# Opening projections accumulated block by block as the conditioning arrives, in a two-layer hybrid backbone

## The chip, the cores and the metric

The kernel runs on one core of a Trainium2 chip. The metric is the device time of one execution in microseconds, as a median over runs; a profiled execution is shown beside it.

## The reference

Two layers over 512 latent tokens and 256 context tokens (768 together), width 1024, in fp32. Each layer has two sub-layers, and each reads a normalised input that is modulated by vectors computed from the conditioning:

```python
mod = jax.nn.silu(c) @ w_ada[layer] + b_ada[layer]            # 1024 -> 6144, and the same for c_ctx
sh1, sc1, gt1, sh2, sc2, gt2 = jnp.split(mod[:, None, :], 6, axis=-1)
h = rmsnorm(x, g_norm1[layer]) * (1 + sc1) + sh1              # the same for the context, with its own mod
p = jnp.split(h @ w_in[layer], SPLIT_POINTS, axis=-1)         # one combined input projection
ya = window_attention(...)    # A: banded attention with rotary
yb = dense_attention(...)     # B: dense attention, normalised q and k, rotary
ym = mlstm_mixer(...)         # C
yd = mamba_mixer(...)         # D
x = x + gt1 * (concat(ya, yb, ym, yd) @ w_out[layer])
h2 = rmsnorm(x, g_norm2[layer]) * (1 + sc2) + sh2
x = x + gt2 * (square(relu(h2 @ w_ff1[layer])) @ w_ff2[layer])
```

So nothing of the input projection can start before the shift and scale (`sh1`, `sc1`) are there. They are the first 2048 columns of `mod`, and the weights for them are 8 MB.

## The kernel before

Activations lie feature-major: `x` is eight chunks of 128 features by 768 tokens (`CTX` the first 256, `LAT` the other 512), held in four double chunks `xr[q]`. Every fp32 operand of a projection is split into a rounded part and a rest (`h`/`hl` for activations, `wh`/`wl` for weights), and a product is three matmuls: high by high, high by low, low by high. `feat` gives a feature-major result of 128 outputs, `tok_group` a token-major one of 128 tokens; each runs over all eight chunks of the contraction and holds one PSUM tile `bulk` (two buffers). `granule(g)` loads 256 output columns of `w_in` through `wload`: DMA into `wraw` (four buffers), ScalarE rounds into `wh`, VectorE subtracts into `wl` (six buffers each). PSUM has besides `bulk` the tags `mx` (two buffers of one bank) and `s2` (two buffers of two banks). Most large tiles share twelve SBUF slots by role (`k6`).

The opening of layer 0. SP issues small constants, then the four loads of `x` (`start_x`), then the conditioning weights. `rms_row` squares on ScalarE, adds on VectorE, sums over partitions by matmuls with ones, and `x` is scaled in place by the row. Then for q = 0 to 3 two sums (`ada_first`) give shift and scale of two chunks. A sum takes 256 columns of `mod` over eight chunks: eight matmuls of 256 columns, each in one of four groups of 32 array columns (`ada_rows`); a ScalarE copy; two transposes, a reduction and the bias (`ada_cols`). Chunks 2q and 2q+1 are then modulated and split into `hs`. After all four rounds the projections run, each over the whole contraction: values for A and B (`G_ABV`, six token groups), keys of A (`G_ABK`), queries of A (`G_AQ`, two halves), each evacuated as it ends (`rotate` applies the rotary by four ScalarE copies of 32 partitions, POOL and VectorE; `put_k` and `put_q` split).

The remaining projections are cut into a stream of small matmul groups (`Stream`, `fill`) that is fed into the attention and scan code by credits. The sixteen other sums of layer 0 (`ada0_step`, columns of `gt1`, `sh2`, `sc2`, `gt2`) are steps in that order: two before and one after the queries of A, six in the stream beside attention A (credit 2.0 each), three and three in the streams beside D and C, one at the end. Each issues its own four loads into `ada` (three buffers), at a priority that lets SP take them as gaps come.

The sums for layer 1 (`ada_step`) run in layer 0's feed-forward on ScalarE and POOL: four loads, ScalarE multiplies by the conditioning, POOL adds (line 292, 294), and at the next step (`ada_finish`) TensorE sums over partitions (line 95, `bulk<-ones,acc`). Of the feed-forward loops `ffn1(b)` calls a step with its second weight block, for b under 2 with its first as well; `ffn2(b)` calls two. All 24 are done before the last pass.

A tile framework orders each engine's instructions by program order and readiness; queues are in order.

Of the kernel before, what the change touches and what calls it, by code (L numbers as in the profile page):

```python
# [43 lines left out]
def tile_hybrid_backbone(ctx, tc, xin, cin, wada, win0, win, wout, wf1, wf2, pcol, prow, cst, rope, out):  # L44
# [77 lines left out]
    SY.dma_start(cc, cin)  # L122
    SY.dma_start(cs, cst)
# [11 lines left out]
    pcs, prs, mods = [], [], []  # L135
    for l in range(DEPTH):
        pcs.append(T((P, NPC), name="pcol"))
        prs.append(T((P, NPR), name="prow"))
        mods.append(T((P, 2, 48), name="mod"))
        SY.dma_start(pcs[l], pcol[l])  # L140
        SY.dma_start(prs[l], prow[l:l + 1, :].to_broadcast([P, NPR]))
# [5 lines left out]
    sth = sm((P, 8, 2), "sth")  # L147
# [28 lines left out]
    def rsq(out_, src, scale, eps):  # L176
        n = src.shape[1]
        v = sm((P, 24), "rv", bufs=2)[:, 0:n]
        y = sm((P, 24), "ry", bufs=2)[:, 0:n]
        w = sm((P, 24), "rw", bufs=2)[:, 0:n]  # L180
# [10 lines left out]
    XIN_ROLES, XOUT_ROLES = (3, 9, 10, 11), (3, 4, 0, 11)  # L191
# [3 lines left out]
    xr = [k6(r, (P, 2, NT), name="x") for r in XIN_ROLES]  # L195
# [4 lines left out]
    def ada_rows(o, kr):  # L200
        for k, w in kr:
            g = slice(32 * (k % 4), 32 * (k % 4) + 32)
            mm(o[g, :], silw[:, 2 * k:2 * k + 32], w, k < 4, k >= 4)

    def ada_cols(l, cb, row, oc):
        for m in range(2):
            TE.transpose(oc[:, m * P:(m + 1) * P], row[:, m * P:(m + 1) * P], ident)
        r = sm((P, 2, 2), "adr", bufs=2)
        V.tensor_reduce(r, oc.rearrange("p (m g i v) -> p v m g i", m=2, g=4, v=2)[:, :, :, :, 0], AX.X, ALU.add)
        tt(mods[l][:, :, 2 * cb:2 * cb + 2], r,  # L210
           pcs[l][:, C_BADA + 2 * cb:C_BADA + 2 * cb + 2].unsqueeze(1).to_broadcast([P, 2, 2]), ALU.add)

    def ada_first(i, cb):
        pt_ = s2()
        o, oc = pt_[:, 0, 0:256], pt_[:, 1, 0:256]
        for kh in range(2):
            if i == 7:
                raws = [T((P, 2, 256), F32, "wraw", 4) for _ in range(2)]
                for q in range(2):
                    SY.dma_start(raws[q], wada[0, cb, kh][:, 2 * q:2 * q + 2, :])  # L220
                ada_rows(o, [(4 * kh + k, raws[k // 2][:, k % 2, :]) for k in range(4)])
            else:
                raw = k6(raw_roles[(2 * i + kh) % 8], (P, 4, 256), name="adaw")
                SY.dma_start(raw, wada[0, cb, kh])
                ada_rows(o, [(4 * kh + k, raw[:, k, :]) for k in range(4)])
        row = tf((P, 256), name="adarow")
# [4 lines left out]
    ada0 = {"i": 8, "pend": None}  # L231

    def ada0_finish():
        if ada0["pend"] is not None:
            cb, row = ada0["pend"]
            ada_cols(0, cb, row, bulk((P, 256)))
            ada0["pend"] = None

    def ada0_step(gate=None):
# [4 lines left out]
        with ExitStack() as st:  # L244
            st.enter_context(tc.high_priority(offset=-1000000))
            if gate is not None:
                st.enter_context(tc.issue_after(gate))
# [3 lines left out]
        o = bulk((P, 256))  # L251
        ada_rows(o, [(k, raws[k // 2][:, k % 2, :]) for k in range(8)])
        row = T((P, 256), F32, "adrow", 2)
        act(row, o, AF.Copy)
        ada0["pend"] = (cb, row)
        ada0["i"] = cb + 1
# [48 lines left out]

    def feat(W, m, acts, sl):
        o = bulk((P, sl.stop - sl.start))
# [177 lines left out]
    for l in range(DEPTH):  # L485
# [11 lines left out]
        if l == 0:  # L497
            hs = new_h()
            def start_x():
                for q in range(4):  # L500
                    SY.dma_start(xr[q], xin[:, 2 * q:2 * q + 2, :])
                for sl in (LAT, CTX):
                    row = rms_row(lambda c: xr[c // 2][:, c % 2, sl], sl.stop - sl.start)
                    for c in range(8):
                        xv = xr[c // 2][:, c % 2, sl]
                        tt(xv, xv, row, ALU.mult)

            start_x()
            for q in range(4):
                for i in range(2):  # L510
                    ada_first(2 * q + i, (4 + q, q)[i])
                for sl, v in ((LAT, 0), (CTX, 1)):
                    s = norm_scale(l, v, C_G1, 8, slice(2 * q, 2 * q + 2))
                    for c in (2 * q, 2 * q + 1):
                        xv, hv = xr[c // 2][:, c % 2, sl], hs[c][0][:, sl]
                        sc, sh = s[:, c:c + 1], md[:, v, c:c + 1]
                        act(hv, xv, AF.Identity, bias=sh, scale=sc)
                        ts(xv, xv, sc, sh, ALU.mult, ALU.add)
                        (G if (c + v) % 2 == 0 else V).tensor_tensor(hs[c][1][:, sl], xv, hv.bitcast(F32), ALU.subtract)
# [180 lines left out]
        W = granule(G_ABV)  # L700
        VS = {a: k6(r, (P, 2, NJ, P), F32R, name="VS") for a, r in (("A", 4), ("B", 5))}
        for j in first_tok:
            o = tok_group(W, j, hs, 256)
            ov = o.rearrange("p (a b v) -> p a b v", a=2, b=2)
            for ai, a in enumerate("AB"):
                act(VS[a][:, :, j, 0:64], ov[:, ai], AF.Copy)
                tt(VS[a][:, :, j, 64:128], ov[:, ai], VS[a][:, :, j, 0:64].bitcast(F32), ALU.subtract)
        W = granule(G_ABK, 0)
        khl["A"] = [k6(r, (P, 2, NT), F32R, name="KHL") for r in (6, 7)]
        pl = feat(W, 0, hs, LAT)  # L710
        put_k(rotate(pl, None, tf((P, NL), name="ra"), rp), khl["A"], LAT)
        put_k(feat(W, 0, hs, CTX), khl["A"], CTX)
        W = granule(G_AQ)
        if l == 0:
            ada0_step(gate=last_dma[0])
            ada0_step()
        for m in range(2):
            eos["A", m] = k6((8, 0)[m], (P, 2, NT), F32R, name="EO")
        for m, sl in snake(segs_out):
            pp = feat(W, m, hs, sl)  # L720
# [16 lines left out]
        def gates():  # L737
            X = sm((P, NJ, 16), "X")
# [92 lines left out]
        astep = [g_do(ada0_step, 2.0)] if l == 0 else []  # L831
        t_ada = 2.0 * len(astep)
# [20 lines left out]
        def ev_conv(i, m, sl):  # L853
            def run(pp):
# [13 lines left out]
                [g_tok(j, hs, 280, ev_z(j)) for j in first_tok] + [gstep] + astep)]  # L868
        for i, g in enumerate((G_DX, G_DB, G_DC)):
# [3 lines left out]
            gs = gs[:len(od) // 2] + [gstep] + (astep if i < 2 else []) + gs[len(od) // 2:] + [gstep]  # L873
            grs.append((lambda g=g: granule(g), gs + astep))
        stream.start(grs, 6 * 2.8 + 4 * (t_lat + t_ctx) + 2 * (t_lat + (t_ctx if need else 0)) + 6 * t_ada)
# [644 lines left out]
```

## Time and profile before

| | |
|---|---|
| median of three runs | 1907.8 us (1907.74 to 1911.45) |
| profiled execution | 1914.86 us, span 1913.1 us |
| TensorE busy | 1796.9 us, 94% of the span |
| VectorE, ScalarE, POOL busy | 1229.7, 869.0, 335.3 us |
| granted TensorE clock, mean | 0.97 |
| DMA | 178.83 MB, mean 93 GB/s |

TensorE's busy time counts pipelined matmuls, so what it stands still is read from waits and from the granted clock by stretches, not from the share. A row of the timeline gives start, length, engine, line, operation and tiles, and in brackets the idle time before it with what ended it. Line 95 is the matmul helper, 103 the activation helper, 106, 110, 111 and 114 VectorE helpers.

### The profile page before, as it was taken

What the parts mean: (1) busy time and instruction counts of PE and PEld (TensorE: products, weight loads), DVE (VectorE), ACT (ScalarE), POOL (GpSimd) and SP (SyncE); (2) the same over time, 40 slices, a digit from 0 to 9 for tenths busy, and PEclk for the clock granted to TensorE, in tenths of its full rate; (3) what the DMA queues carried; (4) which work ended last, traced back from release to release, by engine and by line L of the source; (5) the groups of instructions that cost most, each with busy time, mean ns of one, the idle gap of its engine ahead of it and who ended that gap; (6) DMA issues with size and microseconds to landing.
All of it is one profiled execution on the core that took longest, in us unless ns stands there. A gap on an engine that the chain in (4) does not pass through costs nothing.

```text
span 1913.1 us, 30450 instructions
## 1 busy us (share of the span) xinstructions
PE 1796.9 (94%) x11370; PEld 1552.7 (81%) x11370; DVE 1229.7 (64%) x2811; ACT 869.0 (45%) x1822; POOL 335.3 (18%) x321
## 2 busy tenths in 40 slices
PE   5899999998999899999999999998998899999997
PEld 2687888777878788888888877988877699999997
DVE  6547768478874456645655657787578765555556
ACT  3445532355655555433543436553355543333333
POOL 1210013031004454412412402013120100000000
PEclk9899999999999899999999999999989999999999
DMA  7413243332013234323423321122222022322322
GB/s 265 128 63 111 68 133 108 102 96 99 28 34 119 80 119 129 113 86 116 130 86 104 116 89 58 35 90 67 78 77 67 28 83 92 98 98 89 97 91 67
DMA packets 98100, 178.83 MB, mean 93 GB/s; under 512 B 10784, under 2 KB 19360, under 8 KB 97952
## 3 DMA queue, kind: packets, MB, share of 16 engines
q1 hardware_dynamic: 97952, 176.88, 28.7%
q8 instruction: 90, 1.47, 0.3%
q14 instruction: 58, 0.48, 0.1%
HBM read 172.51 MB, written 4.33 MB: 92 GB/s over the span
## 4 chain that ended last, share of the span: by engine, by line
PE 77%; DVE 8%; ACT 5%; DMA 4%; issue 3%; POOL 2%; SPq 0%; DVEq 0%; ACTq 0%; POOLq 0%
PE bulk L95 40%; PE s L95 26%; PE mx L95 8%; PE mx L658 2%; DMA CB<-drows 1%; DMA ada<-in_wada_dram 1%; DMA adar<-in_wada_dram 1%; POOL acc L292 1%; ACT wh L103 1%; DVE wl L106 1%; ACT qs L103 1%; DMA adaw<-in_wada_dram 1%; DMA wraw<-in_wout_dram 1%; ACT adap L103 1%; DVE x L114 0%
## 5 line engine op out<-in xcount | busy, mean ns | idle before, releaser
L103 ACT ACTIVATE wh<-wraw 128x512 fp32r<-128x512 f32 (+2 forms) x400 | 241.2, 612 | 306.4 <-PE bulk L95 152.4
L106 DVE TENSOR_TENSOR wl<-wraw,wh 128x512 fp32r<-128x512 f32 (+2 forms) x400 | 282.5, 712 | 114.0 <-ACT wh L103 105.1
L95 PE MATMUL s<-h,wh 128*128 128x258 f32 (+2 forms) x1024 | 311.6, 314 | 0.0
L95 PE MATMUL s<-hl,wh 128*128 128x258 f32 (+2 forms) x1024 | 301.1, 312 | 0.0
L95 PE MATMUL s<-h,wl 128*128 128x258 f32 (+2 forms) x1024 | 247.4, 313 | 0.0
L95 PE MATMUL bulk<-ah,wh 128*128 128x512 f32 (+1 forms) x576 | 218.7, 380 | 1.1 <-DVE x L114 0.6
L114 DVE SCALAR_TENSOR_TENSOR x<-bulk,mod,x 128x512 f32<-128x512 f32 (+1 forms) x224 | 149.6, 672 | 107.0 <-PE bulk L95 106.4
L95 PE MATMUL bulk<-al,wh 128*128 128x512 f32 (+1 forms) x576 | 217.2, 377 | 0.0
L95 PE MATMUL bulk<-ah,wl 128*128 128x512 f32 (+1 forms) x576 | 216.9, 376 | 0.0
L292 POOL TENSOR_TENSOR acc<-acc,adap 128x512 f32<-128x512 f32 x96 | 141.3, 1479 | 413.3 <-ACT acc L103 220.7
L95 PEld LDWEIGHTS s<-h,wh 128*128 128x128 f32 x1024 | 195.5, 191 | 20.7
L95 PEld LDWEIGHTS s<-hl,wh 128*128 128x128 f32 x1024 | 195.7, 191 | 11.4
L95 PE MATMUL bulk<-h,wh 128*128 128x512 f32 (+1 forms) x448 | 166.3, 371 | 2.1 <-DVE fD L114 0.7
L95 PEld LDWEIGHTS s<-h,wl 128*128 128x128 f32 x1024 | 164.2, 191 | 1.3
L95 PE MATMUL bulk<-hl,wh 128*128 128x512 f32 (+1 forms) x448 | 156.9, 350 | 0.0
L95 PE MATMUL bulk<-h,wl 128*128 128x512 f32 (+1 forms) x448 | 156.8, 350 | 0.0
L95 PEld LDWEIGHTS bulk<-ah,wh 128*128 128x128 f32 x576 | 109.1, 189 | 21.8 <-DVE mod L106 1.3
L95 PEld LDWEIGHTS bulk<-ah,wl 128*128 128x128 f32 x576 | 108.9, 189 | 21.2
L95 PEld LDWEIGHTS bulk<-al,wh 128*128 128x128 f32 x576 | 108.8, 189 | 19.5
L95 PE MATMUL bulk<-wh,h 128*128 128x256 f32 (+1 forms) x368 | 115.3, 315 | 6.3 <-DVE fD L114 3.2
L103 ACT ACTIVATE relu<-relu,bs 128x512 f32<-128x512 f32 x96 | 59.0, 647 | 117.3 <-DVE relu L106 117.1
L95 PE MATMUL bulk<-wl,h 128*128 128x256 f32 (+1 forms) x368 | 110.0, 300 | 2.0 <-DVE wl L106 1.9
(329 smaller groups left out, 3786.5 us busy)
## 6 DMA issues: line engine op xcount, KB each, us to landing
wraw<-in_wf_dram SPq DMA_DIRECT2D x256, 256.0 KB, 2.8
adar<-in_wada_dram SPq DMA_DIRECT2D x96, 256.0 KB, 3.1
wraw<-in_win_dram SPq DMA_DIRECT2D x80, 256.0 KB, 2.9
ada<-in_wada_dram SPq DMA_DIRECT2D x64, 256.0 KB, 3.4
wraw<-in_wout_dram SPq DMA_DIRECT2D x32, 256.0 KB, 2.9
adaw<-in_wada_dram SPq DMA_DIRECT2D x14, 512.0 KB, 10.5
x<-in_xin_dram SPq DMA_DIRECT2D x8, 768.0 KB, 6.0
CB<-drows SPq DMA_DIRECT2D x10, 512.0 KB, 6.1
```

Source lines behind the costliest of these rows:

```text
L95: return TE.matmul(o, lhsT=l, rhs=r, start=start, stop=stop)
L103: return S.activation(o, i, f, scale=scale, **kw)
L106: return V.tensor_tensor(o, a, b, op)
L114: return V.scalar_tensor_tensor(o, a, s, b, op0, op1)
L292: G.tensor_tensor(acc[:, v], acc[:, v], dst, ALU.add)
L658: TE.transpose(tp[:, i, e, :], Ps[e][:, (i0 + i) * P:(i0 + i + 1) * P], ident)
```

## The change

1. `x` is loaded first; the constants are issued between its parts, layer 1's columns after the first round.
2. The root mean square: ScalarE squares, TensorE sums directly with ones in four groups of 32 columns over all chunks, two ScalarE copies, four transposes, one reduction and `rsq` for both token kinds, six matmuls that spread the row, two ScalarE copies into `rowx`. `x` is no longer scaled in place; `norm_chunk` multiplies by scale and row, adds the shift and splits; odd chunks on POOL.
3. A conditioning sum takes sixteen matmuls of 128 columns in four groups instead of eight of 256; its result is 128 by 128, with one transpose.
4. The first projections run per block q of the contraction: two chunks' worth of values for A and B, keys of A and the first half of the queries of A, into `pav` and `pf`, which hold both `s2` and both `bulk` buffers. Their weights come in a new array `wopen`, one load pair per block. In program order the conditioning of round q+1 stands ahead of block q's matmuls. The second half of the queries follows in `mx`, after the evacuations are issued.
5. The later sums of layer 0: `ada0_load` issues the four loads (four buffers) ahead of `ada0_step`; `spread` places loads and steps evenly in the streams (eight beside A, three, three), credit 1.2 each; one step stands before attention A.
6. The sums of layer 1: a step per `ffn1(b)` for every b, two per `ffn2(b)`, so the last two fall into the last `ffn2`.
7. Small tiles: one buffer instead of two in `rsq`, `bs` two instead of four, `X` and `sth` in shared tags.

```diff
+    for q in range(4):
+        SY.dma_start(xr[q], xin[:, 2 * q:2 * q + 2, :])
+        if q == 0:
+            SY.dma_start(cc, cin)
+        if q == 1:
+            SY.dma_start(cs, cst)
+        if q == 2:
+            load_cols(0)
...
-    def ada_rows(o, kr):
-        for k, w in kr:
-            g = slice(32 * (k % 4), 32 * (k % 4) + 32)
-            mm(o[g, :], silw[:, 2 * k:2 * k + 32], w, k < 4, k >= 4)
+    def ada_rows(o, k, w):
+        for g in range(4):
+            i, m = g % 2, g // 2
+            mm(o[32 * g:32 * g + 32, :], silw[:, 2 * (k + i):2 * (k + i) + 32], w[:, i, m * P:(m + 1) * P], k == 0, k == 6)
...
+    def ada0_load():
+        cb = ada0["i"]
+        if cb < 24 and ada0["raws"] is None:
+            ada0["raws"] = [T((P, 2, 256), F32, "ada", 4) for _ in range(4)]
+            for q in range(4):
+                SY.dma_start(ada0["raws"][q], wada[0, cb, q // 2][:, 2 * (q % 2):2 * (q % 2) + 2, :])
...
-            raws = [T((P, 2, 256), F32, "ada", 3) for _ in range(4)]
-            for q in range(4):
-                SY.dma_start(raws[q], wada[0, cb, q // 2][:, 2 * (q % 2):2 * (q % 2) + 2, :])
...
+            ssq = mx()
...
+            for q in range(4):
+                sq = [k3((P, NT), F32, name="sq") for _ in range(2)]
+                for i in range(2):
+                    act(sq[i], xr[q][:, i, :], AF.Square)
+                for i in range(2):
+                    for g, sl in ((i, LAT), (2 + i, CTX)):
+                        mm(ssq[32 * g:32 * g + 32, 0:sl.stop - sl.start], ones.to_broadcast([P, 32]), sq[i][:, sl], q == 0, q == 3)
...
+            pav, pf = [s2(), bulk()], [s2(), bulk()]
+
+            def cond(q):
                 for i in range(2):
                     ada_first(2 * q + i, (4 + q, q)[i])
-                for sl, v in ((LAT, 0), (CTX, 1)):
+
+            cond(0)
+            load_cols(1)
+            for q in range(4):
+                for i, (sl, v) in enumerate(((LAT, 0), (CTX, 1))):
                     s = norm_scale(l, v, C_G1, 8, slice(2 * q, 2 * q + 2))
                     for c in (2 * q, 2 * q + 1):
...
+                        norm_chunk(xr[c // 2][:, c % 2, sl], sl, s[:, c:c + 1], md[:, v, c:c + 1], rows[i], *hs[c], pool=c % 2 == 1)
+                W = wload([wopen[i, q] for i in range(2)])
+                WT, WF = W[:2], W[2:]
+                if q < 3:
+                    cond(q + 1)
+                else:
+                    ada0_load()
+                for k in (2 * q, 2 * q + 1):
+                    ah, al = hs[k]
+                    h, lo = WT[k % 2]
+                    for j in first_tok:
...
+                        mm(o, ah[:, js], h, k == 0 and j % 2 == 0, False)
+                        mm(o, ah[:, js], lo, False, False)
+                        mm(o, al[:, js], h, False, k == 7 and j % 2 == 1)
+                    h, lo = WF[k % 2]
...
         if l == 0:
+            W = wload([win[l, G_AQ, kh][:, :, P:256] for kh in range(2)])
+            v_ab(pav[1], 0, 2)
+            put_k(pf[1][:, 0:256], khl["A"], CTX)
+            q_a(0, CTX, pf[1][:, 256:512])
+            put_k(rotate(pf[0][:, 0, :], None, tf((P, NL), name="ra"), rp), khl["A"], LAT)
+            q_a(0, LAT, pf[0][:, 1, :])
+            for i in range(2):
+                v_ab(pav[0][:, i, :], 2 + 2 * i, 2)
+            for sl in (LAT, CTX):
+                q_a(1, sl, feat(W, 0, hs, sl, mx))
             ada0_step()
...
-        astep = [g_do(ada0_step, 2.0)] if l == 0 else []
-        t_ada = 2.0 * len(astep)
+        t_ada = 1.2 if l == 0 else 0.0
+
+        def spread(gs, n):
+            if l > 0:
+                return gs
+            res = []
+            for i, g in enumerate(gs):
+                for s in range(n):
+                    if i == (2 * s + 1) * len(gs) // (2 * n):
+                        res.append(g_do(ada0_load))
+                res.append(g)
+                for s in range(n):
+                    if i + 1 == (s + 1) * len(gs) // n:
+                        res.append(g_do(ada0_step, t_ada))
+            return res
...
-                if l == 0 and (cb or b < 2):
+                if l == 0 and cb:
                     ada_step()
```

More of the change, by code (lines that the diff above doesn't have):

```diff
@@ L121, in tile_hybrid_backbone, with load_cols @@
     cc = sm((P, 8, 2), "cc")
-    SY.dma_start(cc, cin)
-    SY.dma_start(cs, cst)
+    slots[0] = tuple(range(12))
+    xr = [k6(r, (P, 2, NT), name="x") for r in (3, 9, 10, 11)]
+    pcs = [T((P, NPC), name="pcol") for _ in range(DEPTH)]
+    prs = [T((P, NPR), name="prow") for _ in range(DEPTH)]
+    def load_cols(l):
+        SY.dma_start(pcs[l], pcol[l])
+        SY.dma_start(prs[l], prow[l:l + 1, :].to_broadcast([P, NPR]))
+    for q in range(4):
[6 more added lines that the diff above has]
+            load_cols(0)
     ident = cs[:, K_ID:K_ID + P]
@@ L133, in tile_hybrid_backbone @@
     mkn = T((P, P), BF16, name="mkn")
[L135 to L141, printed above, removed]
+    mods = [T((P, 2, 48), name="mod") for _ in range(DEPTH)]
     silw = sm((P, 48), "silw")
@@ L213, in ada_first @@
     def ada_first(i, cb):
-        pt_ = s2()
-        o, oc = pt_[:, 0, 0:256], pt_[:, 1, 0:256]
+        pt_ = mx((P, 256))
+        o, oc = pt_[:, 0:P], pt_[:, P:256]
         for kh in range(2):
[L217 to L226, printed above, removed]
+            raw = k6(raw_roles[(2 * i + kh) % 8], (P, 4, 256), name="adaw")
+            SY.dma_start(raw, wada[0, cb, kh])
+            for k in range(0, 4, 2):
+                ada_rows(o, 4 * kh + k, raw[:, k:k + 2, :])
+        row = T((P, P), F32, "adrow", 2)
         act(row, o, AF.Copy)
         ada_cols(0, cb, row, oc)
-    ada0 = {"i": 8, "pend": None}
+    ada0 = {"i": 8, "raws": None, "pend": None}
+    def ada0_load():
[4 more added lines that the diff above has]
+                SY.dma_start(ada0["raws"][q], wada[0, cb, q // 2][:, 2 * (q % 2):2 * (q % 2) + 2, :])
     def ada0_finish():
@@ L235, in ada0_finish, with ada0_step @@
             cb, row = ada0["pend"]
-            ada_cols(0, cb, row, bulk((P, 256)))
+            ada_cols(0, cb, row, bulk((P, P)))
             ada0["pend"] = None
-    def ada0_step(gate=None):
+    def ada0_step():
         ada0_finish()
@@ L243, in ada0_step @@
             return
[L244 to L247, printed above, removed]
-            raws = [T((P, 2, 256), F32, "ada", 3) for _ in range(4)]
-            for q in range(4):
-                SY.dma_start(raws[q], wada[0, cb, q // 2][:, 2 * (q % 2):2 * (q % 2) + 2, :])
-        o = bulk((P, 256))
-        ada_rows(o, [(k, raws[k // 2][:, k % 2, :]) for k in range(8)])
-        row = T((P, 256), F32, "adrow", 2)
+        o = bulk((P, P))
+        for q in range(4):
+            ada_rows(o, 2 * q, ada0["raws"][q])
+        row = T((P, P), F32, "adrow", 2)
         act(row, o, AF.Copy)
-        ada0["pend"] = (cb, row)
-        ada0["i"] = cb + 1
+        ada0.update(i=cb + 1, raws=None, pend=(cb, row))
     ada_state = {"i": 0, "pend": None}
@@ L304, in ada_step, with feat @@
         ada_state["i"] = cb + 1
-    def feat(W, m, acts, sl):
-        o = bulk((P, sl.stop - sl.start))
+    def feat(W, m, acts, sl, tile=bulk):
+        o = tile((P, sl.stop - sl.start))
         ms = slice(m * P, (m + 1) * P)
@@ L497, in tile_hybrid_backbone @@
         if l == 0:
-            hs = new_h()
[L499 to L509, printed above, removed]
+            ssq = mx()
@@ new lines, in tile_hybrid_backbone @@
+            act(ssr[0:64], ssq[0:64], AF.Copy)
+            act(ssr[64:P, 0:NX], ssq[64:P, 0:NX], AF.Copy)
+            sst = mx()
+            for b in range(4):
+                TE.transpose(sst[:, b * P:(b + 1) * P], ssr[:, b * P:(b + 1) * P], ident)
+            rj = sm((P, 2, 4), "rj")
+            V.tensor_reduce(rj, sst.rearrange("p (b s i w) -> p s b i w", b=4, s=2, i=2)[:, :, :, :, 0], AX.X, ALU.add)
+            rjf = rj.rearrange("p s b -> p (s b)")[:, 0:6]
+            rsq(rjf, rjf, 1.0 / 1024.0, EPS)
@@ L510, in tile_hybrid_backbone @@
+            prow_ = s2()
+            for j in range(NJ):
+                mm(prow_[:, j // 4, (j % 4) * P:(j % 4 + 1) * P], rjf[:, j:j + 1].to_broadcast([P, P]), ident)
+            rowx = k4((P, NT), name="rowx")
+            rows = [rowx[:, LAT], rowx[:, CTX]]
+            act(rows[0], prow_[:, 0, :], AF.Copy)
+            act(rows[1], prow_[:, 1, 0:NX], AF.Copy)
+            hs = new_h()
+            pav, pf = [s2(), bulk()], [s2(), bulk()]
+            def cond(q):
                 for i in range(2):
@@ L1463, in _arrange @@
              np.concatenate([run(384, 128), run(896, 128)])]
+    r["wopen"] = np.stack([w[0][:, c] for c in (order[10], np.concatenate([order[8][0:128], order[7][0:128]]))])
+    r["wopen"] = r["wopen"].reshape(2, 4, 2, 128, 256).transpose(0, 1, 3, 2, 4)
     r["win"] = blocks(w[:, :, np.concatenate(order)], 256)
```

98 lines of the change are left out of this document (53 added, 45 removed).

## The prediction

> **What bounds the kernel now.** I read the chain of work that ended last first, then the busy time by stretches, then TensorE's waits, then the timeline of the opening. The chain says who sets the end:
>
> ```profile
> PE 77%; DVE 8%; ACT 5%; DMA 4%; issue 3%; POOL 2%; SPq 0%; DVEq 0%; ACTq 0%; POOLq 0%
> ```
>
> TensorE holds 77% of the chain, and its matmul work is not cut by this change. What can be won is the time in which TensorE stands or runs at a low clock, so I look for where that lies. Columns below: stretch, its length, then busy us (instructions) of PE, PEld, DVE, ACT, POOL, granted clock, DMA share, GB/s.
>
> ```profile
> 0.00:20.00 20.00, 2.92 (x14) 2.12 (x18) 6.38 (x18) 7.62 (x15) 0.37 (x7) 1.00 0.74 289
> 20.00:40.00 20.00, 17.48 (x120) 7.87 (x116) 15.81 (x59) 7.21 (x16) 1.27 (x1) 1.00 0.89 320
> 40.00:60.00 20.00, 13.39 (x85) 9.51 (x86) 18.23 (x42) 10.94 (x22) 10.26 (x7) 0.74 0.31 93
> 60.00:80.00 20.00, 19.88 (x145) 18.65 (x144) 5.19 (x15) 6.96 (x18) 0.00 (x0) 1.00 0.33 106
> 80.00:111.00 31.00, 25.43 (x138) 17.11 (x136) 14.18 (x28) 14.49 (x32) 5.45 (x4) 0.89 0.39 118
> ```
>
> The first 40 us are a DMA stage (share 0.74 and 0.89): x and 8 MB of conditioning weights. In 40 to 60 VectorE is the bound (18.23 of 20) and TensorE's clock is 0.74. Only 60 to 80 is dense; 80 to 111 is holed again. TensorE's waits up to 125 us (us in total, times, longest) name the holes:
>
> ```profile
> PE s L95 <- DMA adaw<-in_wada_dram: 17.1, 1, 17.1
> PE s L207 <- ACT adarow L103: 5.5, 6, 2.2
> PE bulk L95 <- DMA ada<-in_wada_dram: 3.9, 2, 2.1
> PE bulk L207 <- ACT adrow L103: 2.7, 1, 2.7
> ```
>
> The DMA queue and the first projection weights, from the timeline:
>
> ```profile
> 3.55 2.16 SPq L501 DMA_DIRECT2D x<-in_xin_dram  x4
> ...
> 5.75 26.29 SPq L224 DMA_DIRECT2D adaw<-in_wada_dram  x14
> ...
> 15.78 1.15 ACT L103 ACTIVATE sq<-x 128x512 f32<-128x512 f32 x2 [0.73 <-DMA x<-in_xin_dram]
> ...
> 45.68 26.28 SPq L168 DMA_DIRECT2D wraw<-in_win_dram  x12
> ```
>
> The first projection weight is asked for only at 45.68, behind all conditioning loads. The prices of TensorE's work, and the mark by which I measure the opening, the first scores of attention A:
>
> ```profile
> 38.69 1.07 PE L95 MATMUL s<-adaw,silw 128*32 128x256 f32 x16
> ...
> 77.24 0.39 PE L95 MATMUL bulk<-h,wl 128*128 128x512 f32 x1
> 77.47 0.28 PE L95 MATMUL bulk<-h,wh 128*128 128x256 f32 x1
> 77.59 0.28 PE L95 MATMUL bulk<-hl,wh 128*128 128x256 f32 x1
> ...
> 110.95 0.71 PE L95 MATMUL s<-KHL,EO 128*128 128x512 f32 x2
> ```
>
> Start to start, a 512-column matmul takes 0.23 us and a 256-column one 0.12 us.
>
> **The change, step by step.** Work that has to be done before the first scores: values for six token blocks, 6 x 24 x 0.12 = 17.0 us; K and two halves of Q, 3 x 24 x (0.23 + 0.12) = 25 us; together 42 us, in both kernels. The change spreads 33.7 us of it over four blocks of the contraction (8.4 us each: 36 matmuls of 256 columns and 12 of 512, then 12 of 256), each as its eighth of the modulation arrives; 8.4 us (second half of Q) stay behind.
>
> Step 1, x first in SP's queue. x is issued at 3.55 now, behind six small loads; then at once. The four small ones that are left between its parts take a little back: the last square moves from 15.78 to about 13.
>
> Step 2, the root mean square on TensorE. Its sums take the place of VectorE's additions; what comes behind is one chain: last square 1.7 (768 wide, from two of 512 in 1.15), sums 2, two ScalarE copies 1, four transposes 1.4, a reduction and eleven small VectorE steps, six row matmuls 1.6, two copies 1. The small steps go by this row of VectorE (mean ns behind the busy us):
>
> ```profile
> L106 DVE TENSOR_TENSOR rw<-ry 128x4 f32<-128x4 f32 (+1 forms) x6 | 0.9, 157 | 0.1
> ```
>
> With the gaps between dependent steps I take 0.2 each, 2.4. Sum 11, so the row stands at about 24. Normalising the first two chunks and splitting the first opening weights on ScalarE (five pieces of about 0.6 before the first matmul) bring the first block to 28.5. The first block's weights and both first rounds of conditioning are x 3.1 MB, constants 0.3, conditioning 4.2 and weights 0.5, 8.1 MB. At the rates of the first two stretches (5.8 MB by 20 us, then 320 GB/s) that is 27, less the 3 us of step 1: 24. So the row decides the start, not the DMA. The last round (13.4 MB) lands at about 41, and TensorE asks for it at about 51: hidden by 10 us. If that cover went, each us late would be a us lost.
>
> Step 3, four blocks on TensorE: 33.7, plus 2 for a cold start, plus two rounds of conditioning that stand in TensorE's queue between the blocks. One sum is 1.07 (the form is new, sixteen matmuls of 128 columns for eight of 256, the same columns; bounds: 0, as the columns are the same, and double, as the instructions are; I take 0, nearest to the row because weight loads run beside), its wait for the ScalarE copy 0.9 (5.5 over 6), its one transpose 0.2: 2.2, four of them 9. VectorE loses two passes over x and an addition per chunk, so its 18.23 of 20 is not met again. Weights of a block are split while the block before computes: ScalarE has 1.2 of splits and some 3 of normalising against 8.4 of matmuls. All blocks done: 28.5 + 33.7 + 2 + 9 = 73.
>
> The cold start goes by the stretch of 40 to 60: a clock of 0.74 there lost 5 us on two starts, so 2 to 3 each, and I take it once because later blocks follow each other. The Trainium skill ("TensorE: Matmul & The Clock Gate", section "HAM oscillation — how this bites in real kernels") says that idle gaps of more than about 3.4 us send the array back to half rate, so that every tile behind such a gap starts cold. The trace's 0.74 agrees; by that rule, were all four blocks to wait so long, the sum would be some 5 us higher, an estimate from the page's window at half rate.
>
> Step 4, to the first scores. The K and first Q halves now come at once, and ScalarE evacuates them. Its rows for one Q half:
>
> ```profile
> 99.13 2.40 ACT L103 ACTIVATE qs<-bulk 32x512 f32<-32x512 f32 x4 [1.67 <-PE bulk L95]
> 101.98 0.77 ACT L103 ACTIVATE EO<-bulk 64x256 fp32r<-64x256 f32 x2 [0.45 <-PE bulk L95]
> 104.29 1.29 ACT L103 ACTIVATE EO<-ra 64x512 fp32r<-64x512 f32 x2 [1.54 <-POOL ra L542]
> ```
>
> Rotations 2 x 2.4, splits of Q 2.1, of K about twice that, two copies of values: 12 to 14 us, and TensorE has 8.4 + 1.3 (second Q half, one sum) beside it. First scores at 73 + 14 = 87, against 110.95: 24 us gained. Bounds: 77 if the evacuation hides and the row is ready at 22; 109 if every block waits its whole turn (normalise 4.5, split 2, conditioning 4.5, compute 8.4, three times over). Only one conditioning sum lies ahead of the scores, not two: 1.5 is paid back later. Net 22.
>
> Step 5, later sums. Of the waits of the whole span, the second row below is what TensorE waits for loads of later sums; its longest piece, 2.1, came before the scores, 6 after.
>
> ```profile
> PE bulk L95 <- POOL acc L294: 10.2, 7, 3.7
> PE bulk L95 <- DMA ada<-in_wada_dram: 8.1, 7, 2.1
> ```
>
> With four buffers for three and the load issued half a stride ahead, all 6 can go, but the attention stage has other waits right behind, so I take half: 3. In SP's queue these loads now take their turn among the weight loads; their buffers are free by the sum before, so nothing queues behind them for long.
>
> Step 6, the second layer's sums: the first two feed-forward passes of layer 0 lose a step each, and the last pass gets two. TensorE waited 10.2 us for POOL's additions there.
>
> ```profile
> 600.00:620.00 20.00, 18.44 (x101) 15.76 (x99) 9.28 (x20) 14.33 (x32) 10.14 (x8) 0.93 0.42 132
> 620.00:640.00 20.00, 18.40 (x91) 15.89 (x91) 8.14 (x19) 11.21 (x25) 7.81 (x7) 0.85 0.24 77
> ...
> 659.30 0.61 PE L95 MATMUL bulk<-ones,acc 128*128 128x1 f32 x4 [3.65 <-POOL acc L294]
> ...
> 678.23 0.61 PE L95 MATMUL bulk<-ones,acc 128*128 128x1 f32 x4 [2.19 <-POOL acc L294]
> ```
>
> The other five, 4.4, go with their steps; of the 3.65 I take half, the 2.19 stays (its step keeps its distance). That is 6.2, and of the clock lost in the two stretches (0.07 and 0.15 of 20, 4.4) I take 4: 10. Bounds 4 and 15. The two late steps meet the layer's end, where late matmuls cover them: 0, up to 3 lost. Fewer buffers for small tiles: 0, same engine in order.
>
> Sum: 22 + 3 + 10 = 35. The profiled execution took 1914.9 us (span 1913.1); the median of the runs shown is 7 lower, 1907.8. So 1880 in a profile, 1873 as median.
>
> **The rivals.** (a) The rounds run one behind the other: block q waits for normalising and splitting, and only then for TensorE. For it: ScalarE and VectorE take both in order. Against: 8.4 us of matmuls cover them. First scores 109; with steps 5 and 6, 1908 - 13 = 1895. (b) The same with three cold restarts of 2.6, from the 0.74 row: 1903. (c) The opening hides wholly, 77, and all of step 5: 1908 - 33 - 6 - 10 = 1859. (d) Slower: the later sums' loads, now in turn on SP, are not there when the sum stands in TensorE's queue.
>
> ```profile
> DMA to landing us min/median/max: 2.4/3.4/8.5
> ```
>
> A whole landing exposed for all fifteen later sums costs 15 x 3.4 = 51: 1924. It decides from 2.6 us a sum on (39 us, the gain and 0.2%). Against: half a stride is some 10 us. (e) Nothing moves: the work displaced from the opening comes back in attention A: 1908.
>
> **How the numbers follow.** Forecast 1873 (1862 to 1885): 0.60; (a) 0.12, (b) 0.06, (c) 0.12, (d) 0.06, (e) 0.04. About 0.2% (4 us) can be told from no change. The range, 1853 to 1897, holds the forecast, (a) and (c): 0.84 less their tails. Faster 0.60 + 0.12 + 0.06 + 0.12 = 0.90, same 0.04, slower 0.06.
>
> **What would show it.** First scores near 87, the first block's matmuls near 28.5, blocks of 8.4 us with under 3 us between, no wait for the opening's conditioning loads behind the first block, a clock near 1 from 32 on; waits for the later sums' loads under 3 us in all; waits for POOL under 5 and the clock over 0.95 in the first feed-forward passes. Wrong: waits between blocks of 5 us or more, a row much later than 24, a hole between the second Q half and the scores of over 8 us, or a new wait at the end of layer 0.

## The result and the profile after

The changed kernel takes 1858.3 us (median of four runs, 1854.57 to 1865.19) against 1908.2 us (1907.74 to 1911.45) measured beside it: a ratio of 0.9739, 95% interval 0.9706 to 0.9772, so 50 us less. Its profiled execution is the slowest of its four runs: 1865.19 us, span 1862.9. Of the other kernels' profiles below, those that share its opening (e2, e3, e7, e9, e10, e11) reach the first scores 2.1 to 4.6 us earlier than it does, at 86.0 to 88.5.

The chain of work that ended last, after:

```profile
PE 79%; DVE 8%; ACT 5%; DMA 3%; issue 2%; POOL 2%; SPq 0%; DVEq 0%; ACTq 0%; POOLq 0%
```

TensorE holds 79% instead of 77%; the shares of DMA and issue went down by a point each. The stretches of the opening, after (columns as in the prediction):

```profile
20.00:40.00 20.00, 17.44 (x177) 12.94 (x177) 11.41 (x35) 7.13 (x16) 2.22 (x2) 0.70 0.87 320
40.00:60.00 20.00, 20.00 (x235) 17.34 (x234) 11.40 (x29) 9.35 (x20) 4.59 (x4) 1.00 0.52 162
60.00:80.00 20.00, 20.00 (x129) 18.09 (x128) 9.40 (x22) 11.12 (x28) 2.87 (x3) 1.00 0.20 51
```

From 40 to 80 us TensorE is busy without a hole at a clock of 1.00; before, that stretch had 13.39 of 20 at 0.74 and then 19.88. VectorE's 18.23 of 20 is gone (11.40). The low clock now lies in 20 to 40 (0.70). In stretches of 5 us from 15 on it reads 0.50, 0.50, 0.65, 0.69 and 0.97, so most of it falls ahead of the first block, on the root mean square and the first sums. TensorE's waits up to 91 us, after:

```profile
PE mx L95 <- ACT sth L103: 6.7, 1, 6.7
PE mx L95 <- ACT sq L103: 2.7, 1, 2.7
PE s L95 <- DVE EO L106: 2.0, 1, 2.0
PE s L95 <- ACT h L103: 1.7, 1, 1.7
```

No row up to 91 us names a DMA: the conditioning is not waited for behind the first block. Of the weights, only the split of the stream's first ones is waited for, 1.4 us in two pieces behind the second half of the queries. The marks of the opening, from the timeline after:

```profile
14.46 1.58 ACT L103 ACTIVATE sq<-x 128x768 f32<-128x768 f32 x2 [1.73 <-DMA x<-in_xin_dram]
...
23.89 2.93 PE L95 MATMUL s<-cst,rj 128*128 128x128 f32 x12
...
26.86 0.87 ACT L103 ACTIVATE rowx<-s 128x512 f32<-128x512 f32 x2 [4.44 <-PE s L95]
...
29.43 0.15 DVE L106 TENSOR_TENSOR mod<-adr,pcol 128x4 f32<-128x4 f32 x1
...
30.39 0.39 PE L95 MATMUL s<-wh,h 128*128 128x256 f32 x1 [1.74 <-ACT h L103]
...
32.94 0.41 PE L95 MATMUL s<-wh,h 128*128 128x256 f32 x1
33.16 0.41 PE L95 MATMUL s<-wl,h 128*128 128x256 f32 x1
...
72.79 0.38 ACT L103 ACTIVATE VS<-s 128x256 fp32r<-128x256 f32 x1 [5.58 <-PE s L95]
...
75.39 0.40 PE L95 MATMUL mx<-h,wh 128*128 128x512 f32 x1
...
90.64 1.22 PE L95 MATMUL s<-KHL,EO 128*128 128x512 f32 x2 [1.98 <-DVE EO L106]
```

The last squares start at 14.46, the row is copied at 26.86 and ready at 27.7, the first block starts at 30.39 and the first evacuation at 72.79. The four blocks end where the second half of the queries begins, at 75.39, and the first scores start at 90.64. The trace records each matmul of the row and of the sums twice: x12 stands for the row's six, and a sum's eight are x16 before, its sixteen x32 after.

Where the time went, by stages of the kernels that the experiments below use (us; each stage ends where the first matmul of the next begins, read from the timelines of the profiled executions; A, D, C are the attention and scan stages of layer 0, "B" is attention B and the output projection, FF the feed-forward, "rest" all of layer 1 behind it):

| | opening | A | D | C | B | FF | rest | span |
|---|---|---|---|---|---|---|---|---|
| before | 111.0 | 133.6 | 94.4 | 98.7 | 133.9 | 570.4 | 771.1 | 1913.1 |
| after | 90.6 | 121.1 | 87.0 | 105.7 | 130.6 | 551.6 | 776.3 | 1862.9 |
| FF steps alone (e1) | 109.8 | 134.0 | 92.7 | 97.2 | 133.7 | 551.4 | 769.0 | 1887.8 |
| later sums + small tiles alone (e4) | 99.9 | 124.1 | 90.6 | 103.7 | 131.1 | 570.1 | 774.4 | 1893.9 |
| all but the opening (e12) | 101.8 | 124.3 | 86.3 | 103.5 | 131.3 | 552.0 | 773.6 | 1872.8 |
| small tiles alone (e8) | 110.0 | 133.6 | 93.8 | 100.1 | 133.9 | 569.9 | 776.4 | 1917.7 |
| after, three buffers (e3) | 87.9 | 125.4 | 90.5 | 105.3 | 134.8 | 552.7 | 776.8 | 1873.4 |
| after, tiles back (e9) | 88.1 | 121.3 | 88.9 | 103.9 | 128.7 | 552.2 | 768.6 | 1851.7 |
| e9 with credit 2.0 (e11) | 86.2 | 126.5 | 86.0 | 99.4 | 128.9 | 552.6 | 770.2 | 1849.8 |

The opening gave 20.4, A 12.5, D 7.4, B 3.3 and FF 18.8; C took 7.0 back and the rest 5.2. A quarter of the gain comes from A, for which the prediction had part of 3 us.

### The profile page after: what moved, and what is told of

Read it like the earlier page. It is cut to its first block, busy times and chain, and to the rows that moved or that the text cites. A ratio compares the mean times of both kernels' runs of the same rounds, so it can differ in the third digit from the quotient of the medians.

```text
span 1862.9 us, 31119 instructions
## 1 busy us (share of the span) xinstructions
PE 1776.5 (95%) x11754; PEld 1556.4 (84%) x11754; DVE 1227.1 (66%) x2765; ACT 866.1 (46%) x1820; POOL 331.4 (18%) x322
## 4 chain that ended last, share of the span: by engine, by line
PE 79%; DVE 8%; ACT 5%; DMA 3%; issue 2%; POOL 2%; SPq 0%; DVEq 0%; ACTq 0%; POOLq 0%
PE bulk L95 39%; PE s L95 29%; PE mx L95 8%; PE mx L706 2%; ACT wh L103 1%; DVE wl L106 1%; DMA CB<-drows 1%; DVE x L114 1%; DMA adar<-in_wada_dram 1%; ACT qs L103 1%; POOL acc L296 1%; ACT pr L103 1%; DMA x<-in_xin_dram 1%; ACT pth L103 0%; DVE EO L106 0%
## 5 line engine op out<-in xcount | busy, mean ns | idle before, releaser
L106 DVE TENSOR_TENSOR wl<-wraw,wh 128x512 fp32r<-128x512 f32 (+2 forms) x400 | 286.5, 721 | 117.1 <-ACT wh L103 109.2
L95 PE MATMUL s<-h,wh 128*128 128x258 f32 (+2 forms) x1040 | 316.6, 314 | 0.0
L95 PE MATMUL s<-hl,wh 128*128 128x258 f32 (+2 forms) x1040 | 305.9, 313 | 0.0
L95 PE MATMUL s<-h,wl 128*128 128x258 f32 (+2 forms) x1040 | 252.1, 312 | 0.0
L95 PE MATMUL bulk<-h,wh 128*128 128x512 f32 (+1 forms) x416 | 154.2, 371 | 0.9 <-DVE KHL L106 0.5
L95 PE MATMUL bulk<-hl,wh 128*128 128x512 f32 (+1 forms) x416 | 145.3, 349 | 0.0
L95 PE MATMUL bulk<-h,wl 128*128 128x512 f32 (+1 forms) x416 | 145.2, 349 | 0.0
L95 PEld LDWEIGHTS bulk<-ah,wh 128*128 128x128 f32 x576 | 108.3, 188 | 25.3 <-DVE mod L106 4.6
L103 ACT ACTIVATE adap<-adar,silw 128x256 f32<-128x256 f32 x192 | 85.0, 497 | 52.5 <-DMA adar<-in_wada_dram 52.5
L95 PE MATMUL bulk<-wh,h 128*128 128x256 f32 (+1 forms) x336 | 105.4, 314 | 3.0 <-ACT h L103 1.7
```

The source lines that it names most:

```text
L95: return TE.matmul(o, lhsT=l, rhs=r, start=start, stop=stop)
L103: return S.activation(o, i, f, scale=scale, **kw)
L106: return V.tensor_tensor(o, a, b, op)
```

## The experiments

**The feed-forward's steps, alone and undone.** e1 is the kernel before with only this edit; e2 is the changed kernel with the old line.

```diff
-                if l == 0 and (cb or b < 2):
+                if l == 0 and cb:
```

> The kernel before with one edit: layer 1's sums take a step in every first feed-forward pass only with the second weight block. The prediction's step 6 says 10 us (1898). The trace of the changed kernel says that layer 0's feed-forward gave back 20 us and lost 1.6 at its end: 1889 to 1891. If TensorE's waits for POOL alone count (10.2 us), it is 1898; if the clock that they cost counts as well, near 1890 and a clock of 1.00 in the first two passes.

> The changed kernel with the old placement of layer 1's sums. By the prediction's step 6 it is 10 us slower than the changed kernel (1868), by the trace's account 19 (1877), and the waits for POOL come back with some 10 us in the same passes. If the gain hung on the new opening, it stays near 1858.

e1: 1890.8 us (ratio 0.9906, 0.9887 to 0.9926), 18 faster than before. e2: 1876.8 us (0.9835, 0.9817 to 0.9852), 18.6 slower than the changed kernel. In both the FF stage moves by 18 to 19, and no other stage by more than 3.5. Its length, TensorE's busy time and clock, before and then in e1:

```profile
571.60:1142.00 570.40, 555.41 (x3217) 483.32 (x3216) 321.04 (x556) 265.43 (x564) 193.50 (x160) 0.98 0.34 108
```

```profile
567.40:1118.80 551.40, 545.48 (x3217) 477.04 (x3215) 329.70 (x556) 264.43 (x564) 194.60 (x160) 1.00 0.34 111
```

Idle time in the stage goes from 15.0 to 5.9 and busy time from 555.4 to 545.5 at the same 3217 matmul records; the clock goes from 0.98 to 1.00. In e2 the wait of before is back among TensorE's waits:

```profile
PE bulk L95 <- POOL acc L298: 9.9, 8, 3.1
```

So moving a step out of each of the first two passes removes the whole wait for POOL, and about as much again in clock.

**The small tiles, alone and given back.** e8 is the kernel before with part 7 alone; e9 is the changed kernel with two buffers in `rsq` again and `X` in a tile of its own (the room comes from `cc` and `rj` in a shared tag and one buffer for `adrow` and `adr`).

```diff
-        v = sm((P, 24), "rv", bufs=2)[:, 0:n]
+        v = sm((P, 24), "rv")[:, 0:n]
...
-            X = sm((P, NJ, 16), "X")
+            X = th_((P, NJ, 16), name="X")
```

> The kernel before with the smaller tiles alone (one buffer instead of two in the reciprocal root, two instead of four for the shift in the feed-forward, two tiles in shared tags). The prediction said 0: 1908. The trace of the changed kernel lost 5 us in layer 1, whose program is the same: if the smaller tiles do that, by another order of instructions, 1913; if it is another cause or a chance of the run, 1908.

> The changed kernel with the reciprocal root's buffers back to two and the gates' tile back to its own (room from one buffer each less for two other small tiles and from two tiles in shared tags). On the old opening the smaller tiles cost 5 to 10 us. If that is a cost of the tiles themselves, it comes back here: 1849 to 1854, with layer 1 from its first scores to the end at 721 us as before instead of 726. If it is a chance of each order of instructions, 1855 to 1861.

e8: 1918.5 us, ratio 1.0052 (1.0038 to 1.0066): slower by some 10 in the median and 4.6 between the profiles. e9: 1853.3 us (1852.54 to 1854.22), ratio 0.972 (0.9703 to 0.9737): 5 faster than the changed kernel. The two intervals meet, but each of its four runs is below the fastest of the changed kernel's. The mixers of layer 1, from the first scores to the feed-forward, before, in e8 and in e9:

```profile
1192.10:1538.20 346.10, 322.32 (x2094) 279.07 (x2094) 264.46 (x707) 173.81 (x378) 58.76 (x65) 0.96 0.21 65
```

```profile
1190.30:1542.00 351.70, 326.17 (x2094) 283.05 (x2094) 266.82 (x707) 173.63 (x378) 59.53 (x65) 0.94 0.20 64
```

```profile
1132.40:1477.00 344.60, 318.36 (x2094) 275.75 (x2094) 265.27 (x707) 173.66 (x378) 58.46 (x65) 0.97 0.20 65
```

The same 2094 matmuls take 346.1, 351.7 and 344.6 us, with TensorE idle for 23.8, 25.5 and 26.2 and a clock of 0.96, 0.94 and 0.97. What is lost is mainly busy time at a lower clock. The stage "rest" bears it out over all fourteen profiles: 772.0 to 776.8 us in the nine with the smaller tiles, 768.6 to 771.1 in the five without. In e8 the instructions of layer 1 have moved against each other: the scan C stage there takes 5 longer and the one behind it 4 less, then 3.7 are lost in front of the feed-forward. Which of the two tiles does it wasn't run apart.

**The later sums.** e4 is the kernel before with part 5 (and part 7, without which it has no room): loads ahead, four buffers, evenly spread steps, one step ahead of attention A instead of three. e3 is the changed kernel with three buffers and the loads issued in the step, the places of the steps kept.

```diff
 # e4, against the kernel before
-            ada0_step(gate=last_dma[0])
-            ada0_step()
+            ada0_load()
...
 # e3, against the changed kernel: in ada0_step
+        with tc.high_priority(offset=-1000000):
+            ada0["raws"] = [T((P, 2, 256), F32, "ada", 3) for _ in range(4)]
+            for q in range(4):
+                SY.dma_start(ada0["raws"][q], ...)
```

> The kernel before with the later sums of layer 0 as in the changed kernel (loads issued ahead, four buffers, spread evenly, one step instead of three before attention A), and with the smaller tiles that make room for it. By the prediction's step 5, 3 us faster, less nothing for small tiles: 1905. If the 16 us that the changed kernel gained between the first scores and the feed-forward come from this, 1892, or 1897 if the smaller tiles cost the 5 us that layer 1 lost. If those 16 come from the opening instead, 1905 to 1910.

> The changed kernel with the later sums' loads issued within the step, as gaps come and into three buffers, as before; positions, credits and forms stay. The prediction's step 5 holds the load ahead worth 3 us: 1861. If the load ahead carries the 20 us that layer 0's streams gained, 1873 to 1878. If the even spreading carries them, 1858 to 1861, and the waits for these loads are short again.

e4: 1891.3 us, ratio 0.991 (0.9891 to 0.9929), 17.6 faster, although it carries the small tiles' loss. e3: 1871.9 us, ratio 0.9822 (0.9803 to 0.984), 13.6 slower than the changed kernel. The prediction's 3 us is out by a factor of five or more, and the timeline before says why:

```profile
80.85 1.06 PE L95 MATMUL bulk<-ada,silw 128*32 128x256 f32 x12 [0.38 <-DVE ra L106]
...
84.01 0.62 PE L95 MATMUL bulk<-ada,silw 128*32 128x256 f32 x4 [2.10 <-DMA ada<-in_wada_dram]
...
112.22 1.06 PE L95 MATMUL bulk<-ada,silw 128*32 128x256 f32 x12 [0.56 <-DVE adr L209]
...
112.89 0.33 SPq L250 DMA_DIRECT2D ada<-in_wada_dram  x1
...
113.79 3.04 SPq L250 DMA_DIRECT2D ada<-in_wada_dram  x3
...
115.84 0.62 PE L95 MATMUL bulk<-ada,silw 128*32 128x256 f32 x4 [1.80 <-DMA ada<-in_wada_dram]
```

Of the four loads of a sum only three have buffers. The fourth goes out (112.89) when the sum has started to free one (112.22), and the last four records of the sum wait for it until 115.84. Every one of the sixteen sums is torn in this way or a worse one. After, fifteen of the sixteen are one piece, and the next one's loads leave while it runs:

```profile
108.06 1.08 PE L95 MATMUL bulk<-ada,silw 128*32 128x128 f32 x32
...
108.55 1.75 SPq L242 DMA_DIRECT2D ada<-in_wada_dram  x4
```

All sixteen sums as one group (busy, mean ns, idle time just before), 75 to 580 us, before, after and in e4:

```profile
L95 PE MATMUL bulk<-ada,silw 128*32 128x256 f32 x256 | 32.4, 434 | 11.0 <-DMA ada<-in_wada_dram 8.1 <-DVE x L114 0.9 <-DVE kcq L1035 0.6
```

```profile
L95 PE MATMUL bulk<-ada,silw 128*32 128x128 f32 x512 | 19.6, 294 | 3.0 <-DVE adr L217 1.7 <-DVE x L114 1.0 <-ACT qT L103 0.2
```

```profile
L95 PE MATMUL bulk<-ada,silw 128*32 128x256 f32 x256 | 20.4, 430 | 3.4 <-DVE adr L209 2.3 <-DVE x L114 0.9
```

Torn, they hold TensorE for 32.4 + 11.0 us; whole, for 19.6 + 3.0, and in e4, with the old form, for 20.4 + 3.4. That is 20 us, against the 8.1 that the list of waits shows: the list has the wait, not that mostly a piece of 1.06 and one of 0.62 stand for a whole of 1.07. A piece's busy time runs to its modelled end, so the 20 is an estimate; what was measured is e4's 17.6. e3 tears the sums again:

```profile
105.30 0.86 PE L95 MATMUL bulk<-ada,silw 128*32 128x128 f32 x24
...
105.79 3.51 SPq L256 DMA_DIRECT2D ada<-in_wada_dram  x4
...
108.48 0.43 PE L95 MATMUL bulk<-ada,silw 128*32 128x128 f32 x8
```

```profile
L95 PE MATMUL bulk<-ada,silw 128*32 128x128 f32 x512 | 22.7, 295 | 5.9 <-DMA ada<-in_wada_dram 3.3 <-DVE adr L217 1.2 <-DVE x L114 1.0
```

Its group holds TensorE for 6 us more than after, and it lost 13.6 in the median; the other half isn't in any named wait and stays open. So of what e4 gave, 13.6 us go with the loads and the fourth buffer; what the new places of the steps gave was not run by itself.

**The opening alone.** e12 is e4 with e1's line: everything of the change but the opening.

> The kernel before with every part of the change except the opening: the later sums loaded ahead and spread, the feed-forward's steps, the smaller tiles; the opening's projections stay whole, each over the full contraction. The distance from here to the changed kernel is what the opening by itself is worth. By the prediction's terms (later sums 3, feed-forward 10, opening 22): 1895 us. By the two parts run alone (later sums with the smaller tiles 17.6 faster, feed-forward 18 faster), if they add: 1872, and the opening is worth some 14. If they overlap, because both only give the clock back in one place: about 1885.

1875.8 us (1874.72 to 1881.7), ratio 0.9838 (0.9811 to 0.9864). The parts add up nearly: e4 and e1 gave 17.6 and 18, together they give 33.1. The opening is worth the distance to the changed kernel, 17.5 us in the medians and 10 between the profiles (the changed kernel's is its slowest run). The first scores, in e4 and in e12:

```profile
99.89 0.74 PE L95 MATMUL s<-KHL,EO 128*128 128x512 f32 x2
```

```profile
101.85 0.74 PE L95 MATMUL s<-KHL,EO 128*128 128x512 f32 x2
```

So of the 20.4 us by which the changed kernel reaches its scores earlier, 9 to 11 come without any block: in time one sum stands ahead of the first scores instead of two, and it isn't torn. The blocks give 11 here (14 against e9's profile).

**What starts the first block.** e5 is the changed kernel without the root mean square; the row is set to 1.

```diff
-            ssq = mx()
 ...
-            act(rows[0], prow_[:, 0, :], AF.Copy)
-            act(rows[1], prow_[:, 1, 0:NX], AF.Copy)
+            G.memset(rowx, 1.0)
```

> The changed kernel without the root mean square of the opening: no squares, no sums over them, no reduction; the row is set to 1 at the start. This leaves out a part of the computation, so its time only says what the row's chain decides. Theory, the prediction's own (the row decides when the first block starts, 30.4 us in the profile, the conditioning is there by then): first matmul of the first block about 25, all marks behind it 4 to 6 earlier, 1853 us. Rival (the conditioning's DMA and sums decide it; the row only lies beside them): first block between 29 and 31, 1858 us, no difference beyond 2 us. Rival (TensorE's clock decides more than the start: without the sums over squares it is colder when the first block starts): first block earlier, but no mark behind 90 us moved by more than 2.

1857.0 us (1853.77 to 1860.17), ratio 0.9729 (0.9706 to 0.9752): not told apart from the changed kernel. The timeline of e5, and its stretches from 25 to 35:

```profile
25.31 0.58 PE L95 MATMUL s<-wh,h 128*128 128x256 f32 x1 [2.01 <-ACT wh L103]
...
26.66 0.42 PE L95 MATMUL s<-wh,hl 128*128 128x256 f32 x1
26.88 0.42 PE L95 MATMUL s<-wh,h 128*128 128x256 f32 x1
...
31.27 0.28 PE L95 MATMUL bulk<-wh,h 128*128 128x256 f32 x1
31.39 0.28 PE L95 MATMUL bulk<-wl,h 128*128 128x256 f32 x1
```

```profile
25.00:30.00 5.00, 4.51 (x29) 3.58 (x30) 2.33 (x4) 1.87 (x5) 1.82 (x2) 1.00 1.04 420
30.00:35.00 5.00, 5.00 (x57) 3.89 (x57) 3.89 (x11) 0.80 (x2) 0.00 (x0) 1.00 1.03 409
```

```profile
85.08 1.22 PE L95 MATMUL s<-KHL,EO 128*128 128x512 f32 x2 [1.98 <-DVE EO L106]
```

The first block starts at 25.3, as the theory of the row says, and what the start wins reaches the scores: 5.1 us at the start and 5.6 at the scores against the changed kernel's profile, 2.5 and 3.0 against e9's (27.86 and 88.1). The time doesn't show it. How long the row holds the block also depends on TensorE's clock ahead of it, and that differs between profiles of one and the same opening. e10 below has e9's opening; its clock reads 1.00 up to 25 us, and there the row's six matmuls (x12) take 1.60 us and not 2.93:

```profile
20.98 1.60 PE L95 MATMUL s<-cst,rj 128*128 128x128 f32 x12 [0.17 <-DVE rj L114]
...
25.79 0.39 PE L95 MATMUL s<-wh,h 128*128 128x256 f32 x1 [1.75 <-ACT h L103]
```

Against e10 the row is worth 0.5 us. The last expectation came true in its first half: without the row the block starts at half rate (0.22 us from start to start, later 0.12), and e10's block has a slow stretch as well. So the row holds the start, by 0.5 to 5 us depending on the clock, and no run shows that the kernel's time hangs on it.

**Order of the evacuations; the last sums earlier.** e6 evacuates keys and the first queries ahead of the values; e7 puts the two late steps of layer 1's sums into the passes 4 and 6.

```diff
 # e6
+            put_k(rotate(pf[0][:, 0, :], None, tf((P, NL), name="ra"), rp), khl["A"], LAT)
+            q_a(0, LAT, pf[0][:, 1, :])
             put_k(pf[1][:, 0:256], khl["A"], CTX)
 # e7
-                if l == 0 and cb:
+                if l == 0 and (cb or b in (4, 6)):
```

> The changed kernel with the evacuations behind the four blocks in another order: rotated keys and the first half of the queries first, then context keys, values, context queries. The prediction's step 4 says that ScalarE's evacuations set the first scores (90.6 in the changed kernel): they move to about 85 and the time to 1853. If the scores wait for something else (the second PSUM pair, POOL's additions), or the time is given back in attention A, 1858.

> The changed kernel with two of layer 1's sums moved from the last second pass of the feed-forward to the first passes 4 and 6. The trace showed 2.8 us of waits for the last sums' results at the layer's end, so 1.5 to 3 us faster: 1856. If two steps 17 us apart bring the waits for POOL back, 1858 or more.

e6: 1858.8 us (0.9748, 0.9726 to 0.977). Its first scores start at 85.8, against 88.4 and 88.5 in e2 and e7, whose first blocks start within 0.2 us of its own. But attention A is then 2 longer (123.0 against 121.1 in both): nothing is won. e7: 1856.4 us (0.9744, 0.9724 to 0.9764): not told apart.

**Towards a better version.** e10 is e9 with e7's line, e11 is e9 with a credit of 2.0 a step.

```diff
-        t_ada = 1.2 if l == 0 else 0.0
+        t_ada = 2.0 if l == 0 else 0.0
```

> The changed kernel with the small tiles of before (two buffers in the reciprocal root, X in a tile of its own) and the two late sums of layer 1 in the feed-forward passes 4 and 6 instead of the last pass. Tiles back gave 1853.3, sums earlier alone 1856.4 against 1858.3. If the two add: 1851 to 1852. If the late sums cost nothing, as the second comparison could not tell: 1853.3.

> The changed kernel with the small tiles of before (1853.3 us) and, in addition, a credit of 2.0 for each later sum in the streams, as before the change, instead of 1.2. It asks why the stage between the end of scan D and scan C's last part is 5 to 7 us longer in every kernel with the later sums loaded ahead (104 to 105.6 us against 98.7), at a granted clock of 0.74. Theory (the lower credit deals the stream out unevenly, so that the scan's own short matmuls stand alone at its end): that stage back to about 99, 1849 us. Rival (the sums' new places do it, at the start and middle of a granule, whatever their credit): the stage stays at 103 to 105 and the time at 1853, within 2.

e10: 1856.3 us (1849.21 to 1857.51), ratio 0.9719 (0.9698 to 0.9741), no better than e9, and the FF stage is 2 longer than there (554.2). With two sums out of the last pass, the following waits of TensorE stand in that stage:

```profile
PE bulk L95 <- DVE mod L106: 3.5, 2, 2.4
PE mx L95 <- DVE rc L114: 2.9, 2, 2.7
```

In e9 the same two are 2.6 and 2.5 us, and a third is 0.7, so the waits explain 0.6 of the 2; the rest stays open.

e11: 1852.0 us (1848.86 to 1854.33), ratio 0.9699 (0.9684 to 0.9714), the fastest kernel of this study, though its interval meets e9's. Scan C, before, after and in e11:

```profile
339.00:437.70 98.70, 97.21 (x722) 78.91 (x723) 62.25 (x187) 43.62 (x88) 22.14 (x21) 0.95 0.35 111
```

```profile
298.70:404.40 105.70, 102.68 (x769) 88.05 (x770) 63.62 (x187) 43.13 (x86) 18.38 (x19) 0.87 0.33 103
```

```profile
298.70:398.10 99.40, 95.61 (x767) 82.28 (x768) 64.10 (x187) 43.39 (x87) 20.19 (x21) 0.93 0.35 108
```

With the old credit the stage is back at 99.4, from 103.9 in e9, and its clock at 0.93, from 0.89 in e9 and 0.87 in the changed kernel. That is the length that the theory of the uneven deal forecast; that the scan's short matmuls stood alone before is not shown. Attention A, which has eight of the steps, went from 121.3 to 126.5, with 32 more matmul records in it: the credit moves work and holes from one stage to the other, and the 1.4 us between the medians can't be told from nothing.

## Why the prediction was right, and by which terms it was not

The forecast was 1873 with 1853 to 1897, and 1858.3 lies in it. It lies below the forecast's own band of 1862 to 1885, in the part that the range owes to rival (c), and (c)'s way did not occur. The sum was 35 and the chip gave 50. Three terms were sized wrongly: by the runs the opening gave 17.5 (22 forecast), the later sums 17.6 with the tiles' loss in it (3), the feed-forward 18 (10). One that was put at nothing isn't. The places where time would be won were named rightly; that the range held with errors of this size, one of them the other way, is partly luck.

Step 1 and 2. The last squares start at 14.46, not 13, because the last part of x was late. From their start to the row 11 us were forecast and 13.3 came, so the row is ready at 27.7, not 24. The prediction booked a cold start at the blocks only; here the row's chain runs at half rate too (clock 0.50 from 15 to 25), and its six matmuls take 2.93 us for the 1.6 taken. In e10, at a clock of 1.00, they take 1.60, and the row is ready at 23.5. The step says that the row decides the start, and e5 bears that out in part. The path is less direct than it was put: the row's matmuls also stand in TensorE's queue ahead of the second half of the second sum, whose shift is ready at 29.43. The first block came at 30.4 for 28.5, but at 27.6 to 28.2 in e2, e3, e6, e7 and e9, and at 25.8 and 26.0 in e10 and e11: 28.5 was close, and the changed kernel's profile is the latest of all.

Step 3. Right. The blocks were to take 44.7 us (33.7 + 2 + 9). They take 45.0 (30.39 to 75.39), and the same in the seven other profiles named above. Their end came at 75.4 for 73 because the start was late; in e2, e3, e6, e7 and e9 it came at 72.6 to 73.3. (The values for six token blocks, 6 x 24 x 0.12, are 17.3 and not 17.0; nothing hangs on it.) The new form of the sum takes 1.08 for 1.07, so the value 0 between its bounds was the right one, and the cold start came once: the 256-column matmuls of the first block start 0.22 us apart at 32.94 and 33.16.

Step 4. 87 was forecast, 14 us behind the blocks; 90.64 came, 15.2 us behind them, and 86.0 to 88.5 in the profiles that share the opening. The evacuation does set the scores, but e6 shows that an earlier start of the scores alone buys nothing. The step's fault is the base: it booked the whole distance from 110.95 to the blocks, where e4 and e12 reach 100 to 102 without them. The two torn sums in the stretch of 80 to 111 were read as waits of 2.1 and 2.7 us; one sum in one piece in their place was worth 9 to 11. So the opening itself gave 17.5 of the 22 in the medians, and 11 to 14 at the mark.

Step 5. The mis-sized term: 3 forecast, 17.6 measured in e4 with the tiles' loss in it (9 to 11 of it lie ahead of the first scores, where step 4 had booked them). The prediction named the fourth buffer, and priced the listed wait alone, halved. The rows that would have told it were there: sixteen sums as x12 and x4.

Step 6. 10 forecast, 18 to 19 measured. It gave half of the 3.65 and all of the 2.19 to remain; the whole wait went. And it counted the clock of two stretches (4.4) where TensorE's busy time in the stage fell by 9.9. Before, the waits around the stretch of 620 to 640, whose clock was 0.85, read in the timeline:

```profile
618.03 0.60 PE L95 MATMUL bulk<-ones,acc 128*128 128x1 f32 x4 [1.33 <-POOL acc L294]
...
620.52 1.02 PE L95 MATMUL bulk<-ones,acc 128*128 128x1 f32 x4 [0.75 <-POOL acc L294]
...
640.13 0.61 PE L95 MATMUL bulk<-ones,acc 128*128 128x1 f32 x4 [1.21 <-POOL acc L294]
```

None is longer than 1.33 us. The Trainium skill ("TensorE: Matmul & The Clock Gate", section "HAM oscillation — how this bites in real kernels") asks that no idle gap exceed about 3.4 us. Here one wait of the seven does (3.65). From 580 to 680 the clock reads 0.97, 0.93, 0.85, 1.00 and 0.83 in stretches of 20 us, and 5.0 of the 8.4 us that this takes lie ahead of that wait: by that rule they would have been missed, so the trace differs. The prediction let the 0.74 of 40 to 60 agree with that rule. The half rate is there, but no wait of TensorE's in that stretch was longer than 2.2 us (its own second row of waits), so the length does not agree there either. The late sums at the end of the layer cost nothing that e7 or e10 could tell, as taken.

Small tiles. Put at 0 with the reason "same engine in order"; they cost 5 (e9) to 10 (e8). The engine is the same, but with a buffer less the work of layer 1 came in another order, and that was for the worse; how the one leads to the other was not followed.

The rivals. (a) and (b) didn't occur: TensorE is busy for 20.00 of 20 in both stretches from 40 to 80. (c) gives almost the measured time, 1859, but not its way: the opening wasn't hidden wholly (first scores at 86 to 91, not 77). (d) is the opposite of what happened in the changed kernel, where no wait for these loads is left; e3 shows its size if the buffers are missing, 13.6 us. (e) failed: attention A became shorter too.

## What to carry to other kernels

Count the pieces, not only the waits: when an operation appears in the timeline as x12 and x4 where one x16 was written, its loads have fewer buffers than pieces, and it costs its engine more than the wait that is listed. Before pricing a restructured stage, take out of its old time what another part of the same change removes there. Fewer buffers for a small tile are not free even on one engine: give the change back by itself and time it, since here that alone was worth some 5 us.

## What the runs showed of the hardware

Waits of 0.5 to 3.7 us, 10.2 us in all, cost about as much again in TensorE's rate: in the feed-forward 9 us of idle time and 9.9 us of busy time went together, at the same 3217 matmul records (e1 against before).

The granted clock doesn't show every slow start. In e5's stretch from 25 to 30 it reads 1.00, and 256-column matmuls start 0.22 us apart there; 5 us later it is 0.12 at the same reading. For a first start the spacing of equal matmuls is the better gauge.

One and the same opening meets different clocks. The row's six matmuls took 2.93 us in the changed kernel's profile (clock 0.50 from 20 to 25) and 1.60 in e10's (1.00), and its first block started at 30.4 and at 25.8.
